# Row variance of 8192 rows: one streaming pass on VectorE, or a sum on VectorE and a square pass on ScalarE over larger DMA pieces

## The chip, the cores and the metric

The kernel runs on one core of a Trainium2 chip. The metric is the time of one execution on the device in microseconds (us). The kernel before has a median of 655.45 us over 10 runs (655.2 to 655.67). The profile quoted here is one execution, recorded by the hardware profiler.

## The reference

The input is 8192 rows of 8192 float32 values, 268.4 MB in all; the output is the (population) variance of each row, 8192 floats.

```python
def setup_inputs():
    return {"x": np.random.randn(8192, 8192).astype(np.float32)}

def reference(x):
    return np.var(x, axis=1)
```

## The kernel before

The rows are cut into 64 tiles of 128 rows, one row per partition. A tile `xt` has 128 x 8192 floats (32 KiB per partition, 4.19 MB) and lives in the pool `data` with four buffers. `issue_dma(t)` loads a tile in two halves of 128 x 4096 floats (16 KiB per partition, 2.1 MB): the first half is issued by SyncE (SP), the second by ScalarE (ACT), each from its own DMA queue (L54). A load into a buffer that was used before waits until VectorE has read the tile that lay there. The loop issues the load of tile `t` ahead of the work on tile `t - 3`.

`compute(t)` is all VectorE (DVE): 16 instructions `bn_stats` (L61), each of which reads 512 floats per partition and leaves six statistics in `st`, then one `bn_aggr` (L63), which merges the 16 groups into mean and variance `mv`. GpSimd (POOL) copies the variance into column `t` of `var_all` (L64). There is no second pass over the data.

Behind the last tile, TensorE (PE) transposes `var_all` (L74) to 64 rows of 128 values in PSUM, ScalarE copies them to SBUF (L76), and one DMA writes them out (L77). No order is written out by hand; each engine runs its instructions in the order of the program and waits on semaphores.

Of the kernel before, what the change touches and what calls it, by code (L numbers as in the profile page):

```python
# [1 line left out]

# [5 lines left out]


@with_exitstack  # L10
def kernel(
    ctx: ExitStack,
    tc: tile.TileContext,
    x: bass.AP,
    out: bass.AP,
):
    nc = tc.nc
    P = 128
    n, m = x.shape

    FMAX = nc.vector.BN_STATS_FMAX
    assert m % FMAX == 0
    nsub = m // FMAX

    assert n % P == 0
    ntiles = n // P

    x_t = x.rearrange("(t p) (s f) -> t p s f", p=P, f=FMAX)
    out_t = out.rearrange("(t p) -> t p", p=P)

    data = ctx.enter_context(tc.tile_pool(name="data", bufs=4))
    stats = ctx.enter_context(tc.tile_pool(name="stats", bufs=8))
    singles = ctx.enter_context(tc.tile_pool(name="singles", bufs=1))
    psum = ctx.enter_context(tc.tile_pool(name="psum", bufs=1, space=bass.MemoryType.PSUM))
    outp = ctx.enter_context(tc.tile_pool(name="outp", bufs=1))

    var_all = singles.tile([P, ntiles], mybir.dt.float32)
    ident = singles.tile([P, P], mybir.dt.float32)
    make_identity(nc, ident)

    dma_eng = [nc.sync, nc.scalar]

    CH = 2
    spc = nsub // CH

    xts = [None] * ntiles
    LOOK = 3

    def issue_dma(t):
        xt = data.tile([P, nsub, FMAX], mybir.dt.float32)  # L50
        for c in range(CH):
            lo = c * spc
            hi = lo + spc
            dma_eng[c % 2].dma_start(out=xt[:, lo:hi, :], in_=x_t[t, :, lo:hi, :])  # L54
        xts[t] = xt

    def compute(t):
        xt = xts[t]
        st = stats.tile([P, nsub, nc.vector.BN_STATS_DIM], mybir.dt.float32)
        for j in range(nsub):  # L60
            nc.vector.bn_stats(out=st[:, j, :], in_=xt[:, j, :])  # L61
        mv = stats.tile([P, nc.vector.BN_AGGR_DIM], mybir.dt.float32)
        nc.vector.bn_aggr(out=mv, in_=st)  # L63
        nc.gpsimd.tensor_copy(out=var_all[:, t : t + 1], in_=mv[:, 1:2])  # L64

    for t in range(ntiles):
        issue_dma(t)
        if t >= LOOK:
            compute(t - LOOK)
    for t in range(ntiles - LOOK, ntiles):  # L70
        compute(t)

    vp = psum.tile([ntiles, P], mybir.dt.float32)
    nc.tensor.transpose(vp, var_all, ident)  # L74
    vs = outp.tile([ntiles, P], mybir.dt.float32)
    nc.scalar.copy(vs, vp)  # L76
    nc.sync.dma_start(out=out_t, in_=vs)  # L77


# [1 line left out]
_INS = ['x']  # L81
_OUTS = [((8192,), 'float32')]


# [23 lines left out]
```

## Time and profile before

| what | value |
|---|---|
| median of 10 runs | 655.45 us (655.2 to 655.67) |
| time of the profiled execution | 655.2 us |
| its span, first to last instruction | 653.4 us |
| DVE busy | 636.2 us (97%) |
| ACT, POOL, PE busy | 1.5, 12.4, 0.4 us |
| moved by the DMA engines | 268.57 MB, mean 411 GB/s over the span |
| DMA queues | two, 48.5% and 48.2% of the 16 engines' span |

The span is 1.8 us shorter than the time of the same execution; that rest lies outside the instructions. A row of the list of instruction groups names the line, the engine, the operation, output and inputs with their shapes, and then the busy time in total and the mean time of one. Instructions in a row can overlap slightly, so that the distance between starts is shorter than the mean time of one.

### The profile page before, as it was taken

To read this page: it belongs to the slowest core of one execution; us is meant where nothing else is said; L and a number is where in the kernel's file an instruction comes from. 1 tells how busy PE (TensorE), PEld (TensorE's weight loads), DVE (VectorE), ACT (ScalarE), POOL (GpSimd) and SP (SyncE) were. 2 spreads that over 40 slices of the span, in tenths; PEclk is the share of its full clock that TensorE was granted. 3 is DMA by queue.
4 is the path that set the end of the run, shared out by engine and by line. 5 is a ranking of instruction groups with operands and counts; after the bars stand their busy time and mean duration, and the time that the engine had idled before them with its cause. 6 is when DMAs were issued, how large, how long until landed. Compare 5 with 4: busy or idle time off the path is not lost.

```text
span 653.4 us, 1512 instructions
## 1 busy us (share of the span) xinstructions
PE 0.4 (0%) x1; PEld 0.1 (0%) x1; DVE 636.2 (97%) x1088; ACT 1.5 (0%) x2; POOL 12.4 (2%) x70
## 2 busy tenths in 40 slices
PE   0000000000000000000000000000000000000000
PEld 0000000000000000000000000000000000000000
DVE  2999999999999999999999999999999999999997
ACT  0000000000000000000000000000000000000000
POOL 0000000000000000000000000000000000000000
DMA  9999999999999999999999999999999999999950
GB/s 369 431 429 425 430 428 428 427 430 428 425 430 429 426 428 430 427 427 429 430 425 429 429 426 426 431 428 425 430 429 426 428 429 428 426 429 429 427 227 3
DMA packets 18524, 268.57 MB, mean 411 GB/s; under 512 B 2064, under 2 KB 2128, under 8 KB 2128
## 3 DMA queue, kind: packets, MB, share of 16 engines
q1 hardware_dynamic: 9296, 134.25, 48.5%
q10 hardware_dynamic: 9216, 134.22, 48.2%
q14 instruction: 12, 0.10, 0.0%
HBM read 268.44 MB, written 0.03 MB: 411 GB/s over the span
## 4 chain that ended last, share of the span: by engine, by line
DVE 88%; DMA 6%; issue 5%; SPq 0%; PE 0%; ACT 0%; POOLq 0%; POOL 0%
DVE st L61 82%; DMA xt<-in_x_dram 6%; DVE mv L63 5%; SPq L54 0%; PE vp L74 0%; ACT vs L76 0%; POOLq L103 0%; POOL var_all L64 0%
## 5 line engine op out<-in xcount | busy, mean ns | idle before, releaser
L61 DVE BATCH_NORM_STATS2 st<-xt 128x6 f32<-128x512 f32 x1024 | 609.9, 670 | 13.4 <-DMA xt<-in_x_dram 13.4
L63 DVE BATCH_NORM_AGGREGATE mv<-st 128x2 f32<-128x96 f32 x64 | 36.4, 568 | 0.1
L64 POOL COPY var_all<-mv 128x1 f32<-128x1 f32 x64 | 11.7, 183 | 636.9 <-DVE mv L63 636.9
L76 ACT ACT_TABLE_LOAD x1 | 1.3, 1283 | 609.7 <-DMA xt<-in_x_dram 609.7
L74 PE MATMUL vp<-ident,var_all 128*64 128x128 f32 x1 | 0.4, 422 | 650.0 <-POOL var_all L64 650.0
L76 ACT COPY vs<-vp 64x128 f32<-64x128 f32 x1 | 0.3, 258 | 39.5 <-PE vp L74 39.5
masks.py:199 POOL TENSOR_SCALAR_AFFINE_SELECT ident<-ident 128x128 f32<-128x128 f32 x1 | 0.3, 292 | 0.1
L74 PEld LDWEIGHTS vp<-ident,var_all 128*64 128x64 f32 x1 | 0.1, 128 | 650.0 <-POOL var_all L64 650.0
masks.py:197 POOL MEMSET ident<- 128x128 f32 x1 | 0.2, 204 | 0.3 <-POOLq L92 0.3
L92 POOL MEMSET const-float32-0.0<- 128x1 f32 x1 | 0.1, 98 | 0.2 <-issue 0.2
L92 POOL MEMSET const-bfloat16-1.0<- 128x1 bf16 x1 | 0.1, 101 | 0.0
L92 POOL MEMSET const-uint8-127<- 128x1 uint8 x1 | 0.1, 101 | 0.0
L92 POOL MEMSET const-float32-1.0<- 128x1 f32 x1 | 0.1, 98 | 0.0
## 6 DMA issues: line engine op xcount, KB each, us to landing
xt<-in_x_dram ACTq DMA_DIRECT2D x64, 2048.0 KB, 29.2
xt<-in_x_dram SPq DMA_DIRECT2D x64, 2048.0 KB, 29.0
out_dram<-vs SPq DMA_DIRECT2D x1, 32.0 KB, 1.9
```

The source lines that it names most:

```text
L61: nc.vector.bn_stats(out=st[:, j, :], in_=xt[:, j, :])
L63: nc.vector.bn_aggr(out=mv, in_=st)
L64: nc.gpsimd.tensor_copy(out=var_all[:, t : t + 1], in_=mv[:, 1:2])
L74: nc.tensor.transpose(vp, var_all, ident)
L76: nc.scalar.copy(vs, vp)
L92: nc = _bacc.Bacc("TRN2", target_bir_lowering=False, num_devices=1)
```

## The change

- **Tiles.** Two adjacent rows lie on one partition. A tile has 128 x 16384 floats (64 KiB per partition, 8.4 MB, one contiguous piece of the input), there are 32 of them, and `data` has three buffers. Each of the tiles 0 to 29 is one DMA on SyncE's queue; ScalarE issues none. Tile 30 comes in three DMAs (row 0; the halves of row 1), tile 31 in 13 pieces: six of 2048 floats per partition, two of 1024, three of 512, two of 256.
- **Tiles 0 to 30, two passes.** VectorE forms a row's sum with one `scalar_tensor_tensor` (`row_sum`), which adds the row's two halves element by element (4096 pairs; the pairs themselves go to the PSUM tile `pair` and aren't used) and accumulates the total in `s`. ScalarE makes the mean with a small ACTIVATE, and then one Square ACTIVATE over the 8192 floats (`row_sq`) with the mean as bias, written in place over the row, which accumulates the squared deviations in `ssq`. Row 1 of tile 30 is summed by halves.
- **Their output.** PE transposes `ssq` for each of the two rows, ScalarE scales by 1/8192 into `vs`, one DMA writes 31 x 256 values.
- **Tile 31.** As before with `bn_stats` and `bn_aggr` on VectorE, except for 2048 floats of row 1: of these ScalarE forms a shifted sum and a shifted sum of squares (Identity and Square, with the mean of the first `bn_stats` group as shift), and four small GpSimd instructions turn them into one more group for `bn_aggr`. The two variances per partition, `var_last`, leave in one last DMA.

The diff, cut to its core (the removed lines are those of the functions above):

```diff
-    data = ctx.enter_context(tc.tile_pool(name="data", bufs=4))
+    x_t = x.rearrange("(t p j) f -> t p (j f)", p=P, j=J)      # J = 2, H = m // 2
+    data = ctx.enter_context(tc.tile_pool(name="data", bufs=3))
+    small = ctx.enter_context(tc.tile_pool(name="small", bufs=4))
...
+    def row_sum(s, i, src, w):
+        nc.vector.scalar_tensor_tensor(
+            out=pair[:, 0 : w // 2], in0=src[:, 0 : w // 2], scalar=1.0, in1=src[:, w // 2 : w],
+            op0=ALU.mult, op1=ALU.add, accum_out=s[:, i : i + 1])
...
+        if k == 1:
+            nc.scalar.activation(out=mean, in_=s[:, 0:1], func=ACTF.Identity, scale=1.0 / m)
...
+        nc.scalar.activation(out=src, in_=src, func=ACTF.Square, bias=mean, scale=-1.0,
+                             accum_out=ssq[:, j, t : t + 1])
...
+    for t in range(NT - 1):
...
+        if last:
+            for lo, hi in ((0, m), (m, m + H), (m + H, 2 * m)):
+                nc.sync.dma_start(out=xt[:, lo:hi], in_=x_t[t, :, lo:hi])
+        else:
+            nc.sync.dma_start(out=xt, in_=x_t[t])
+        for j in range(J):
...
+                row_sum(s, 0, rows[j], m)
+                row_sq(s, 1, rows[j], t, j)
...
+    for w in [2048] * 6 + [1024, 1024, 512, 512, 512, 256, 256]:
+        nc.sync.dma_start(out=xt[:, lo : lo + w], in_=x_t[t, :, lo : lo + w])
+        lo += w
...
+        nc.tensor.transpose(vp, ssq[:, j, 0 : NT - 1], ident)
+        nc.scalar.mul(vs[:, :, j], vp, 1.0 / m)
+    nc.sync.dma_start(out=out_tj[0 : NT - 1], in_=vs)
...
+    nc.scalar.activation(out=junk, in_=src, func=ACTF.Identity, bias=k, scale=-1.0, accum_out=s12[:, 0:1])
+    nc.scalar.activation(out=junk, in_=src, func=ACTF.Square, bias=k, scale=-1.0, accum_out=s12[:, 1:2])
...
+    for i, w in enumerate([512] * 7 + [256, 256]):
+        bn(st1, 4 + i, lo, w)
+        lo += w
+    mv1 = small.tile([P, 2], FP32, name="mv1")
+    nc.vector.bn_aggr(out=mv1, in_=st1)
+    nc.vector.tensor_copy(out=var_last[:, 1:2], in_=mv1[:, 1:2])
+        nc.sync.dma_start(out=out_last[t], in_=var_last)
```

How the instructions stand now on two engines. On VectorE, the kernel before begins with the first tile like this (`st` and `mv` are the statistics, DMAHW the semaphores of the loads), and goes on so to its end:

```order
L61 BN_STATS st<-xt 128x6 [waits DMAHW1_49]
L61 BN_STATS st<-xt 128x6 x7
L61 BN_STATS st<-xt 128x6 [waits DMAHW0_49]
L61 BN_STATS st<-xt 128x6 x7
L61 BN_STATS st<-xt 128x6 [waits DMAHW3_49]
L63 BN_AGGR mv<-st 128x2 [waits DVE_49]
```

The scheduler puts a tile's `bn_aggr` behind the first `bn_stats` of the next. The whole VectorE program of the changed kernel, from tile 0 to the end, with the statistics of tile 31's two rows as `st_474` and `st_492`:

```order
L49 SCALAR_TENSOR_TENSOR pair,s<-xt 128x4096 x61
L49 SCALAR_TENSOR_TENSOR pair,s<-xt 128x2048 x2
L101 BN_STATS st_474<-xt 128x6 x16
L128 BN_AGGR mv_491<-st_474 128x2
L101 BN_STATS st_492<-xt 128x6 x13
L135 BN_AGGR mv_517<-st_492 128x2
L136 COPY var_last<-mv_517 128x1
```

Of 1024 `bn_stats`, 29 are left, and 63 pair sums stand ahead of them. On SyncE's queue the 64 half-row loads (ScalarE's queue had 64 more) become whole tiles, and both output DMAs stand behind the last piece:

```order
-L54 DMA xt<-in_x_dram 128x4096 x64
-L77 DMA out_dram<-vs 64x128
-L103 UNCONDITIONAL_BRANCH
+L164 UNCONDITIONAL_BRANCH
+L73 DMA xt<-in_x_dram 128x16384 x30
+L71 DMA xt<-in_x_dram 128x8192
+L71 DMA xt<-in_x_dram 128x4096 x2
+L89 DMA xt<-in_x_dram 128x2048 x6
+L89 DMA xt<-in_x_dram 128x1024 x2
+L89 DMA xt<-in_x_dram 128x512 x3
+L89 DMA xt<-in_x_dram 128x256 x2
+L98 DMA out_dram<-vs 31x256
```

The row of the last output, `out_dram<-var_last 128x2`, follows these. Eight semaphores serve all loads in turn, so that a DMA also waits until the one eight places ahead of it has landed. ScalarE, which issued 64 loads and copied once, now runs 62 pairs of a mean and a Square over 8192 floats, then the two scalings into `vs`, then the two passes over 2048 floats.

More of the change, by code (lines that the diff above doesn't have):

```diff
@@ L7 @@
 from concourse._compat import with_exitstack
+FP32 = mybir.dt.float32
+ACTF = mybir.ActivationFunctionType
+ALU = mybir.AluOpType
 @with_exitstack
@@ L19 @@
     n, m = x.shape
[L21 to L29, printed above, removed]
-    data = ctx.enter_context(tc.tile_pool(name="data", bufs=4))
-    stats = ctx.enter_context(tc.tile_pool(name="stats", bufs=8))
+    F = nc.vector.BN_STATS_FMAX
+    J = 2
+    NT = n // (P * J)
+    H = m // 2
+    x_t = x.rearrange("(t p j) f -> t p (j f)", p=P, j=J)
@@ L33 @@
+    out_tj = out.rearrange("(t q) -> t q", q=P * J)
+    out_last = out.rearrange("(t p j) -> t p j", p=P, j=J)
+    data = ctx.enter_context(tc.tile_pool(name="data", bufs=3))
+    stats = ctx.enter_context(tc.tile_pool(name="stats", bufs=1))
+    small = ctx.enter_context(tc.tile_pool(name="small", bufs=4))
     singles = ctx.enter_context(tc.tile_pool(name="singles", bufs=1))
     psum = ctx.enter_context(tc.tile_pool(name="psum", bufs=1, space=bass.MemoryType.PSUM))
-    outp = ctx.enter_context(tc.tile_pool(name="outp", bufs=1))
@@ L37 @@
-    var_all = singles.tile([P, ntiles], mybir.dt.float32)
-    ident = singles.tile([P, P], mybir.dt.float32)
+    ssq = singles.tile([P, J, NT], FP32)
+    var_last = singles.tile([P, J], FP32)
+    pair = psum.tile([P, H], FP32)
+    ident = singles.tile([P, P], FP32)
     make_identity(nc, ident)
[L41 to L77, printed above, removed]
+    def row_sum(s, i, src, w):
+        nc.vector.scalar_tensor_tensor(
+            out=pair[:, 0 : w // 2], in0=src[:, 0 : w // 2], scalar=1.0, in1=src[:, w // 2 : w],
+            op0=ALU.mult, op1=ALU.add, accum_out=s[:, i : i + 1])
@@ new lines, in row_sq @@
+    def row_sq(s, k, src, t, j):
+        mean = small.tile([P, 1], FP32, name="mean")
+        if k == 1:
+            nc.scalar.activation(out=mean, in_=s[:, 0:1], func=ACTF.Identity, scale=1.0 / m)
+        else:
+            parts = small.tile([P, 4], FP32, name="parts")
+            nc.scalar.activation(out=parts[:, 0:k], in_=s[:, 0:k], func=ACTF.Identity, scale=1.0 / m,
+                                 accum_out=mean)
+        nc.scalar.activation(out=src, in_=src, func=ACTF.Square, bias=mean, scale=-1.0,
+                             accum_out=ssq[:, j, t : t + 1])
@@ new lines @@
+    for t in range(NT - 1):
+        xt = data.tile([P, J * m], FP32, name="xt")
+        rows = [xt[:, j * m : (j + 1) * m] for j in range(J)]
+        last = t == NT - 2
+        if last:
+            for lo, hi in ((0, m), (m, m + H), (m + H, 2 * m)):
+                nc.sync.dma_start(out=xt[:, lo:hi], in_=x_t[t, :, lo:hi])
+        else:
+            nc.sync.dma_start(out=xt, in_=x_t[t])
+        for j in range(J):
+            s = small.tile([P, 2], FP32, name="s")
+            if last and j == J - 1:
+                row_sum(s, 0, rows[j][:, 0:H], H)
+                row_sum(s, 1, rows[j][:, H:m], H)
+                row_sq(s, 2, rows[j], t, j)
+            else:
+                row_sum(s, 0, rows[j], m)
+                row_sq(s, 1, rows[j], t, j)
@@ new lines @@
+    t = NT - 1
+    xt = data.tile([P, J * m], FP32, name="xt")
+    lo = 0
+    for w in [2048] * 6 + [1024, 1024, 512, 512, 512, 256, 256]:
+        nc.sync.dma_start(out=xt[:, lo : lo + w], in_=x_t[t, :, lo : lo + w])
+        lo += w
+    vs = singles.tile([NT - 1, P, J], FP32)
+    for j in range(J):
+        vp = pair[0 : NT - 1, j * F : j * F + P]
+        nc.tensor.transpose(vp, ssq[:, j, 0 : NT - 1], ident)
+        nc.scalar.mul(vs[:, :, j], vp, 1.0 / m)
+    nc.sync.dma_start(out=out_tj[0 : NT - 1], in_=vs)
@@ new lines, in bn @@
+    def bn(st, i, lo, w):
+        nc.vector.bn_stats(out=st[:, i * 6 : i * 6 + 6], in_=xt[:, lo : lo + w])
+    st0 = stats.tile([P, m // F * 6], FP32, name="st0")
+    for c in range(m // F):
+        bn(st0, c, c * F, F)
+    mv0 = small.tile([P, 2], FP32, name="mv0")
+    NA = 2048
+    st1 = stats.tile([P, 13 * 6 + 3], FP32, name="st1")
+    b = 13 * 6
+    s12 = small.tile([P, 2], FP32, name="s12")
+    tmp = small.tile([P, 2], FP32, name="tmp")
+    nc.gpsimd.memset(st1[:, b : b + 1], float(NA))
@@ new lines @@
+    bn(st1, 0, m, F)
+    k = st1[:, 1:2]
+    src = xt[:, m + NA : m + 2 * NA]
+    junk = pair[:, NA : 2 * NA]
+    nc.scalar.activation(out=junk, in_=src, func=ACTF.Identity, bias=k, scale=-1.0, accum_out=s12[:, 0:1])
+    nc.scalar.activation(out=junk, in_=src, func=ACTF.Square, bias=k, scale=-1.0, accum_out=s12[:, 1:2])
+    nc.gpsimd.tensor_scalar(out=tmp[:, 0:1], in0=s12[:, 0:1], scalar1=1.0 / NA, scalar2=0.0,
+                            op0=ALU.mult, op1=ALU.add)
+    nc.gpsimd.tensor_tensor(out=st1[:, b + 1 : b + 2], in0=k, in1=tmp[:, 0:1], op=ALU.subtract)
@@ new lines @@
+    nc.gpsimd.tensor_tensor(out=tmp[:, 1:2], in0=s12[:, 0:1], in1=tmp[:, 0:1], op=ALU.mult)
+    nc.gpsimd.tensor_tensor(out=st1[:, b + 2 : b + 3], in0=s12[:, 1:2], in1=tmp[:, 1:2], op=ALU.subtract)
+    for i in range(1, 4):
+        bn(st1, i, m + i * F, F)
+    nc.vector.bn_aggr(out=mv0, in_=st0)
+    nc.gpsimd.tensor_copy(out=var_last[:, 0:1], in_=mv0[:, 1:2])
+    lo = m + 2 * NA
+    for i, w in enumerate([512] * 7 + [256, 256]):
+        bn(st1, 4 + i, lo, w)
+        lo += w
+    mv1 = small.tile([P, 2], FP32, name="mv1")
@@ L81 @@
+    nc.vector.bn_aggr(out=mv1, in_=st1)
+    nc.vector.tensor_copy(out=var_last[:, 1:2], in_=mv1[:, 1:2])
+    with nc.allow_non_contiguous_dma(reason="two values per partition"):
+        nc.sync.dma_start(out=out_last[t], in_=var_last)
 _INS = ['x']
```

## The prediction

> **What bounds the kernel now.** I read the page first, then the waits, then the timeline at both ends, then the DMA rate by stretches. The page:
>
> ```profile
> span 653.4 us, 1512 instructions
> PE 0.4 (0%) x1; PEld 0.1 (0%) x1; DVE 636.2 (97%) x1088; ACT 1.5 (0%) x2; POOL 12.4 (2%) x70
> DMA  9999999999999999999999999999999999999950
> DMA packets 18524, 268.57 MB, mean 411 GB/s; under 512 B 2064, under 2 KB 2128, under 8 KB 2128
> q14 instruction: 12, 0.10, 0.0%
> L61 DVE BATCH_NORM_STATS2 st<-xt 128x6 f32<-128x512 f32 x1024 | 609.9, 670 | 13.4 <-DMA xt<-in_x_dram 13.4
> L63 DVE BATCH_NORM_AGGREGATE mv<-st 128x2 f32<-128x96 f32 x64 | 36.4, 568 | 0.1
> L64 POOL COPY var_all<-mv 128x1 f32<-128x1 f32 x64 | 11.7, 183 | 636.9 <-DVE mv L63 636.9
> L76 ACT COPY vs<-vp 64x128 f32<-64x128 f32 x1 | 0.3, 258 | 39.5 <-PE vp L74 39.5
> masks.py:197 POOL MEMSET ident<- 128x128 f32 x1 | 0.2, 204 | 0.3 <-POOLq L92 0.3
> L92 POOL MEMSET const-float32-0.0<- 128x1 f32 x1 | 0.1, 98 | 0.2 <-issue 0.2
> out_dram<-vs SPq DMA_DIRECT2D x1, 32.0 KB, 1.9
> ```
>
> Two things look full: VectorE (97%) and the DMA engines (9 in every slice until the last two). The waits tell which one leads. VectorE waited for data only 13.4 us, three times, 13.0 of it before the first tile:
>
> ```profile
> DVE st L61 <- DMA xt<-in_x_dram: 13.4, 3, 13.0
> SPq L54 <- DVE st L61: 571.4, 60, 9.8
> ```
>
> SyncE's queue waits for VectorE to free a buffer before 60 of its loads. So VectorE sets the end. Its beginning, one tile's turn, and its end:
>
> ```profile
> 12.98 9.59 DVE L61 BATCH_NORM_STATS2 st<-xt 128x6 f32<-128x512 f32 x16 [12.98 <-DMA xt<-in_x_dram]
> ...
> 629.67 0.57 DVE L63 BATCH_NORM_AGGREGATE mv<-st 128x2 f32<-128x96 f32 x1
> ...
> 639.61 0.57 DVE L63 BATCH_NORM_AGGREGATE mv<-st 128x2 f32<-128x96 f32 x1
> 640.09 8.93 DVE L61 BATCH_NORM_STATS2 st<-xt 128x6 f32<-128x512 f32 x15
> 649.13 0.59 DVE L63 BATCH_NORM_AGGREGATE mv<-st 128x2 f32<-128x96 f32 x1
> 650.76 0.56 SPq L77 DMA_DIRECT2D out_dram<-vs  x1
> ```
>
> From one `bn_aggr` to the next is 9.94 us: a tile costs VectorE 9.94 us, 64 tiles 636 us. The DMA side by stretches (the last two columns are the busy share of the DMA engines and GB/s):
>
> ```profile
> 0.00:5.00 5.00, 0.00 (x0) 0.00 (x0) 0.00 (x0) 0.00 (x0) 0.70 (x6) 1.00 0.67 226
> 5.00:15.00 10.00, 0.00 (x0) 0.00 (x0) 2.02 (x4) 0.00 (x0) 0.00 (x0) 1.00 1.02 436
> 7.00:17.00 10.00, 0.00 (x0) 0.00 (x0) 4.02 (x7) 0.00 (x0) 0.00 (x0) 1.00 0.99 424
> 15.00:605.00 590.00, 0.00 (x0) 0.00 (x0) 589.54 (x1009) 0.00 (x0) 10.82 (x59) 1.00 1.01 428
> 628.00:629.00 1.00, 0.00 (x0) 0.00 (x0) 1.00 (x2) 0.00 (x0) 0.00 (x0) 1.00 0.86 361
> 629.00:630.00 1.00, 0.00 (x0) 0.00 (x0) 1.00 (x3) 0.00 (x0) 0.00 (x0) 1.00 0.20 82
> ```
>
> The DMA engines run at 428 GB/s from start to end with a share of 1.01, although the buffers are freed at VectorE's pace (4.194 MB in 9.94 us would be 422 GB/s). They are full in their own right and merely a little faster: 4.194 MB at 428 GB/s is 9.80 us a tile. The first stretch dates the start of the stream: 226 GB/s times 5 us is 1.13 MB, 2.64 us at 428, so it began at 2.36 us. 268.44 MB at 428 GB/s are 627.2 us, which ends at 629.6, as the last two rows show. So the gap between the bounds is small: a kernel bound by this stream saves about the 20 us between 629.6 and VectorE's last instruction, less its own tail.
>
> **The change part by part.** My sum is: start of the stream, stream, tail; it holds if the engines are covered.
>
> *VectorE, tiles 0 to 30.* 992 `bn_stats` and 62 `bn_aggr` go; 62 row sums come. No row shows a pair sum. The nearest is `bn_stats`: 15 in 8.93 us are 595 ns for 512 floats, 1.16 ns per element. A row sum of 4096 pairs at one pair per such step is 4.8 us; at two reads per pair in turn, 9.5 us. I take 4.8, and keep 9.5 as a rival. A tile of two rows then asks 9.5 us of VectorE in the 19.4 us that its data stream.
>
> *ScalarE.* Per row a mean (one small instruction: the copy of 128 elements, 258 ns) and a Square over 8192. The only ScalarE row, 258 ns for 128, would give 2.02 ns per element if it had no fixed part, 16.5 us per row. GpSimd's two fills, 204 ns for 128 and 98 ns for 1, give 0.835 ns per element, 6.8 us. GpSimd's copy of one single element takes 183 ns, so most of the 258 is fixed, and I take 6.8 + 0.26 = 7.1 us; with the mean 7.4, 14.7 us a tile of 19.4. The upper end is a rival.
>
> *Buffers.* Three instead of four, but of double size. Landing and start (0.8 us, below), first sum 4.8, mean and Square 7.4, again 7.4 (the second sum lies beneath the first Square): a buffer is free 20.4 us after its tile has streamed. By then one tile is just streaming and the load for the freed buffer is needed at 38.7 us, so 18 us are left. Costs nothing; it would cost if ScalarE needed more than 9.7 us per row.
>
> *Queue.* All loads move from two queues to SyncE's. ScalarE loses its 64 issues, SyncE has 46 for 64. Each waits for a buffer, and the two or three loads ahead of it cover that. In tile 31 a piece waits for the landing of the one eight places ahead; when piece 9 may go, pieces 2 to 8 (14.6 us of data) still stand in the queue. Nothing.
>
> *The stream.* This is the term that decides. The trace has payload packets of 16 KiB only: 18524 less the 2128 small ones and the 12 of queue 14 (instructions), 16384, or 1024 per DMA engine. At the bulk rate the stream is 627.2 us; at the best stretch's 436 it is 615.7. If the 11.5 us between are lost between packets, each costs 11.2 ns. The changed kernel, with one packet per partition and piece, has 30 x 8 + 3 x 8 + 13 x 8 = 368 packets per engine, 4.1 us: 619.8 us. The ends are 615.7 and 627.2. The bulk row is the longest, but it stands for the old packets; I take 619.8. It assumes the 436 isn't merely what a 10 us window counts at its edges; the 424 two microseconds later warns of that.
>
> The Trainium skill, page DMA: Bandwidth & Descriptors, sections Bandwidth, Measured and Where 436 GB/s comes from, puts the ceiling at 435.2 GB/s and a packet at about 10.5 ns. By it the stream would be 616.8 + 368 x 10.5 ns = 620.7 us, and the total 0.9 us above mine. The trace agrees as far as it goes: a 16 KiB packet takes 612.5 ns at 428 GB/s and 602.4 at that ceiling, 10.1 ns apart.
>
> *End of the stream.* 2.36 + 619.8 = 622.2. The rows from 628 to 630 (0.86, then 0.20) show that the engines don't end together; I add 0.5: 622.7.
>
> *Tail.* The first tile's data were through at 2.36 + 9.80 = 12.16 and VectorE began at 12.98: 0.82 us. The last `bn_stats` of 256 is 0.30, and VectorE at 1.16 ns per float against 1.19 of the stream may be one such behind, 0.30. `bn_aggr` 0.59; the copy to `var_last` as GpSimd's, 0.18; two handovers, 0.1; the output DMA from its issue to the end as before, 653.4 - 650.76 = 2.64. Together 4.9. Hidden: the output of the first 31 tiles (issued behind the last piece; 0 to 1.9 us if the last output stood behind it) and ScalarE's 2048 floats: piece 6 lands 15.4 us after tile 30's stream, two passes 3.9, four GpSimd steps 0.8, 20.1 against 21.9 for VectorE's last `bn_stats`.
>
> Sum: 622.7 + 4.9 = 627.6 us span. Outside the span 1.8 us (655.2 - 653.4): 629.4. The median of the runs is 0.25 above the profiled execution: **629.7 us**.
>
> **The rivals.**
>
> *Same rate.* The 428 is the chip's rate for any packet length here, and 436 an edge effect. For it: it holds over 590 us; 424 stands beside 436. Against: the share of 1.01 with the same packets in the best stretch. The stream stays 627.2: 7.4 more, 637.1 us.
>
> *Two reads in turn.* A pair sum takes 9.5 us. VectorE then needs 19.0 of 19.4 us a tile, still covered, but at the end it is late: tile 30's last half is summed 10.1 us after its stream, row 0 of tile 31 done at 20.1, the rest (11 `bn_stats` of 512, two of 256) at 27.3 instead of 21.9. 5.4 more: 635.1 us. Nothing in the trace of before speaks to it, since no instruction there has two inputs. The Trainium skill, page Vector Engine (DVE) Microarchitecture Reference, section Points that are easy to get wrong, says that this instruction shape with two float32 SBUF sources halves its throughput; no run so far shows it.
>
> *ScalarE becomes the bound.* With x for mean and Square of a row, the end is first landing 22.6 + first sum 4.8 + 62 x + about 9.4 (scaling, two passes, GpSimd, `bn_aggr`, output). It binds from 9.7, and the kernel is slower than before from (653.4 - 36.8) / 62 = 9.94 us. At 16.5 + 0.26 it would be 1076 us of span, about 1078. For it only the row of 258 ns taken without a fixed part; against it the 0.835 ns slope.
>
> **How the numbers follow.** The forecast has 0.66, the same rate 0.17, two reads 0.10, ScalarE 0.03, the rest (two of them together, a rate below 428) 0.04. The forecast's own range is 627.5 to 632 (stream 617.7 to 621; tail up to 1.5 longer). The range of 8 in 10 must reach the same rate and two reads: 628 to 637.6. All but ScalarE and part of the rest are faster than 654.1, by more than the 0.2% that can be told from no change: faster 0.94, within 0.2% 0.02, slower 0.04.
>
> **What would show it.** About 6,800 packets instead of 18,524; a bulk rate near 432 GB/s (428 means same rate; 18,524 packets would mean that the pieces are cut again); VectorE about half busy and waiting for DMA, its pair sums 4.8 us (9.5: two reads); ScalarE's Square near 7.1 us, the engine some 73% busy; loads issued one tile ahead of need; the last `bn_stats` 1.4 us behind the stream. The prediction falls if the DMA share drops below 9 in mid-run, which would mean a late buffer, or if the gap between the last landing and the end is far from 4.9 us.

## The result, and the profile after

The changed kernel takes 632.94 us (median of 8 runs, 632.71 to 633.38) against 655.36 us of the kernel before (29 runs). The ratio is 0.966 (95% interval 0.9651 to 0.9668): faster by 3.4%, as forecast; the time lies inside the range and 3.2 us above the 629.7 that was named. The profiled execution has a span of 631.2 us. Its page, the lines that answer to those of before:

```profile
span 631.2 us, 589 instructions
PE 0.8 (0%) x2; PEld 0.3 (0%) x2; DVE 297.2 (47%) x158; ACT 462.3 (73%) x194; POOL 1.6 (0%) x12
DMA  9999999999999999999999999999999999999995
DMA packets 6805, 268.51 MB, mean 425 GB/s; under 512 B 881, under 2 KB 1168, under 8 KB 1808
L62 ACT ACTIVATE xt<-xt,mean 128x8192 f32<-128x8192 f32 x62 | 441.5, 7121 | 2.0
L49 DVE SCALAR_TENSOR_TENSOR pair<-xt 128x4096 f32<-128x4096 f32 (+1 forms) x63 | 275.0, 4365 | 327.9 <-ACT xt L62 277.3
L57 ACT ACTIVATE mean<-s 128x1 f32<-128x1 f32 x61 | 11.9, 195 | 158.4 <-DVE pair L49 158.4
L101 DVE BATCH_NORM_STATS2 st<-xt 128x6 f32<-128x512 f32 (+1 forms) x29 | 17.3, 660 | 1.9 <-DMA xt<-in_x_dram 1.8
```

VectorE went from 97% to 47%, ScalarE from nothing to 73%, and the DMA engines are full until the last slice. No engine is near its limit any more: the stream of the input is what is left. The 277 us that VectorE waits for ScalarE (L49, last column) cost nothing by themselves: it waits for work that isn't needed earlier. In time, the bulk and the end of the stream (busy share of the DMA engines and GB/s at the right):

```profile
15.00:600.00 585.00, 0.00 (x0) 0.00 (x0) 274.65 (x123) 437.66 (x179) 0.00 (x0) 1.00 1.00 432
...
622.00:623.00 1.00, 0.00 (x0) 0.00 (x0) 1.00 (x3) 0.97 (x3) 0.52 (x3) 1.00 0.98 334
623.00:624.00 1.00, 0.00 (x0) 0.00 (x0) 1.00 (x3) 1.00 (x1) 0.00 (x0) 1.00 0.21 76
624.00:625.00 1.00, 0.00 (x0) 0.00 (x0) 1.00 (x2) 0.33 (x2) 0.19 (x1) 1.00 0.06 19
625.00:626.00 1.00, 0.00 (x0) 0.00 (x0) 1.00 (x4) 0.00 (x0) 0.00 (x0) 1.00 0.00 0
```

432 GB/s instead of 428, held over 585 us. Most DMA engines are through by 623.5 us; a share of 0.06 is one of the 16, and the last packet ends at 624.8. What comes behind the stream, in order of time:

```profile
621.34 5.01 DVE L101 BATCH_NORM_STATS2 st<-xt 128x6 f32<-128x512 f32 x9 [0.83 <-DMA xt<-in_x_dram]
626.45 0.52 DVE L135 BATCH_NORM_AGGREGATE mv<-st 128x2 f32<-128x81 f32 x1
627.00 0.15 DVE L136 COPY var_last<-mv 128x1 f32<-128x1 f32 x1
627.25 0.36 SPq L138 DMA_DIRECT2D out_dram<-var_last  x1
```

VectorE works without a gap from 621.34 to 626.35, so it ends 1.6 us behind the last packet; the output DMA then takes 631.2 - 627.25 = 3.95 us to the end. Before the change it took 2.64.

### The profile page after: what moved, and what is told of

The parts are those of the page before. It is cut to its first block, busy times and chain, and to the rows that moved or that the text cites. A ratio compares the mean times of both kernels' runs of the same rounds, so it can differ in the third digit from the quotient of the medians.

```text
span 631.2 us, 589 instructions
## 1 busy us (share of the span) xinstructions
PE 0.8 (0%) x2; PEld 0.3 (0%) x2; DVE 297.2 (47%) x158; ACT 462.3 (73%) x194; POOL 1.6 (0%) x12
## 4 chain that ended last, share of the span: by engine, by line
ACT 58%; DMA 22%; DVE 19%; issue 0%; SPq 0%; DVEq 0%
ACT xt L62 57%; DMA xt<-in_x_dram 22%; DVE pair L49 18%; ACT mean L57 1%; DVE st L101 1%; DVE mv L135 0%; SPq L73 0%; SPq L71 0%; DVE var_last L136 0%; DVEq L49 0%; DVEq L135 0%
## 5 line engine op out<-in xcount | busy, mean ns | idle before, releaser
L62 ACT ACTIVATE xt<-xt,mean 128x8192 f32<-128x8192 f32 x62 | 441.5, 7121 | 2.0
L49 DVE SCALAR_TENSOR_TENSOR pair<-xt 128x4096 f32<-128x4096 f32 (+1 forms) x63 | 275.0, 4365 | 327.9 <-ACT xt L62 277.3
L57 ACT ACTIVATE mean<-s 128x1 f32<-128x1 f32 x61 | 11.9, 195 | 158.4 <-DVE pair L49 158.4
L101 DVE BATCH_NORM_STATS2 st<-xt 128x6 f32<-128x512 f32 (+1 forms) x29 | 17.3, 660 | 1.9 <-DMA xt<-in_x_dram 1.8
L62 ACT ACTIVATION_READ_ACCUMULATOR xt<-xt,mean 128x1 f32 x62 | 11.6, 187 | 0.0
L49 DVE DVE_READ_ACCUMULATOR pair<-xt 128x1 f32 x63 | 8.9, 142 | 0.0
L119 ACT ACTIVATE pair<-xt,st 128x2048 f32<-128x2048 f32 x1 | 2.0, 1971 | 0.5 <-DMA xt<-in_x_dram 0.5
L120 ACT ACTIVATE pair<-xt,st 128x2048 f32<-128x2048 f32 x1 | 2.0, 1971 | 0.0
L128 DVE BATCH_NORM_AGGREGATE mv<-st 128x2 f32<-128x96 f32 x1 | 0.6, 589 | 0.0
```

Source lines behind the costliest of these rows:

```text
L49: nc.vector.scalar_tensor_tensor(out=pair[:, 0 : w // 2], in0=src[:, 0 : w // 2], scalar=1.0, in1=src[:, w // 2 : w], op0=ALU.mult, op1=AL ...
L57: nc.scalar.activation(out=mean, in_=s[:, 0:1], func=ACTF.Identity, scale=1.0 / m)
L62: nc.scalar.activation(out=src, in_=src, func=ACTF.Square, bias=mean, scale=-1.0, accum_out=ssq[:, j, t : t + 1])
L101: nc.vector.bn_stats(out=st[:, i * 6 : i * 6 + 6], in_=xt[:, lo : lo + w])
L119: nc.scalar.activation(out=junk, in_=src, func=ACTF.Identity, bias=k, scale=-1.0, accum_out=s12[:, 0:1])
L120: nc.scalar.activation(out=junk, in_=src, func=ACTF.Square, bias=k, scale=-1.0, accum_out=s12[:, 1:2])
```

## Experiments

All times are medians; the kernel before was run beside each group and stayed at 655.33 to 655.36 us, so the groups can be compared. Each expectation was written before its run.

**Rows apart: half the packet length, the same number of DMAs.**

```diff
+    x_a = x.rearrange("(t j p) f -> t p j f", p=P, j=J)
...
-            nc.sync.dma_start(out=xt, in_=x_t[t])
+            nc.sync.dma_start(out=xt.rearrange("p (j f) -> p j f", j=J), in_=x_a[t])
...
```

> The changed kernel, but the two rows of a partition are 128 rows apart in the input (tiles 0 to 30), so that each tile is still one DMA, of two 32 KiB packets per partition instead of one of 64. Theory A (each packet costs the DMA engines about 10 ns, whatever its length): 240 packets more per engine, +2.4 us, 635.3 us against 632.9. Theory B (the rate of 432 GB/s comes from one queue or from whole-tile DMAs, packet length does not matter): 632.9.

Measured: 635.35 us (635.04 to 635.53), +2.4. Theory A, to the tenth. Its bulk rate is 431 GB/s with 10645 packets.

**Quarters: the old packet length on the one queue.**

```diff
-            nc.sync.dma_start(out=xt, in_=x_t[t])
+            for lo in range(0, J * m, 4096):
+                nc.sync.dma_start(out=xt[:, lo : lo + 4096], in_=x_t[t, :, lo : lo + 4096])
```

> The changed kernel, but tiles 0 to 29 come in four DMAs of 16 KiB per partition each, the packet length of the kernel before, all from SyncE's queue. Theory A (10 ns per packet): 720 data packets and 90 completions more per engine, +7.3 to +8.2 us, 640 to 641 us, bulk rate 428 GB/s as before the change. Theory B (one queue instead of two gave the rate): 632.9 us and 432 GB/s.

Measured: 639.41 us (639.27 to 639.52), +6.5, below the 7.3 to 8.2 of theory A, far from B. The bulk rate is back at that of before:

```profile
5.00:100.00 95.00, 0.00 (x0) 0.00 (x0) 40.43 (x18) 63.47 (x26) 0.00 (x0) 1.00 1.00 428
100.00:600.00 500.00, 0.00 (x0) 0.00 (x0) 229.11 (x102) 377.28 (x154) 0.00 (x0) 1.00 1.01 428
```

The landing itself can be read from SyncE's issues in tile 31: the issue of piece 8 waits for tile 30's last piece. These three rows are of the changed kernel, of rows apart, and of quarters:

```profile
604.15 0.33 SPq L89 DMA_DIRECT2D xt<-in_x_dram  x1
```
```profile
606.57 0.33 SPq L90 DMA_DIRECT2D xt<-in_x_dram  x1
```
```profile
611.71 0.33 SPq L90 DMA_DIRECT2D xt<-in_x_dram  x1
```

+2.42 us for 240 packets more per engine is 10.1 ns each; +7.56 us for 720 is 10.5 (90 completions included in the time, not in the count). The 10.5 is too high: before this landing all five instruction packets of quarters have crossed a DMA engine, but only three of the changed kernel's five, and each holds an engine up (see the late second piece below). Over the whole time, with five in both, quarters is 6.47 us slower, 9.0 ns a packet. In rows apart three stand ahead of the landing, as in the changed kernel. So packet length makes the rate, at 9 to 10 ns a packet. The 1.1 us that quarters gives back behind this point comes up below.

**An eighth of the work.**

```diff
...
-                row_sum(s, 0, rows[j], m)
-                row_sq(s, 1, rows[j], t, j)
+                row_sum(s, 0, rows[j][:, 0:1024], 1024)
+                row_sq(s, 1, rows[j][:, 0:1024], t, j)
```

> The changed kernel with one eighth of the work on tiles 0 to 30: sums and squares run over 1024 floats of each row only (the rest of the row is left out of the result). Theory (the stream alone sets the time, the engines are covered): 632.9 us within 0.4. Rival (ScalarE's late release of buffers, or VectorE's late start on tile 31, still costs something): 1 to 3 us faster.

Measured: 632.83 us (632.50 to 632.94), the same. ScalarE at 15% and VectorE at 10% buy nothing: in the changed kernel both lie wholly under the stream, and their traffic doesn't slow it.

**The new loads alone, with the old work on VectorE.**

```diff
...
+        nc.sync.dma_start(out=xt, in_=x_t[t])
+        for j in range(J):
...
+                nc.vector.bn_stats(out=st[:, c * 6 : c * 6 + 6], in_=xt[:, lo : lo + F])
...
+            nc.vector.bn_aggr(out=mv, in_=st)
...
```

> The new loads alone: 32 tiles of two rows per partition, one DMA of 64 KiB per partition each on SyncE's queue, three buffers, but bn_stats and bn_aggr on VectorE for every row as before the change. Theory (VectorE at 9.94 us per row was the bound, and a tile of double size starts it 10 us later): 22.7 + 636.2 + about 4.6 of tail = 663.5 us span, 665 us, slower than before. Rival (the larger pieces are the gain): below 640 us.

Measured: 670.09 us (669.99 to 670.13), 2.25% slower than before (ratio 1.0225, 1.0211 to 1.0238). The direction and its cause are as expected, the size was 5 us short:

```profile
L73 DVE BATCH_NORM_STATS2 st<-xt 128x6 f32<-128x512 f32 x1024 | 609.8, 674 | 22.6 <-DMA xt<-in_x_dram 22.6
L75 DVE BATCH_NORM_AGGREGATE mv<-st 128x2 f32<-128x96 f32 x64 | 37.1, 580 | 3.2
```

VectorE waits 22.6 us for the first tile of double size instead of 13.0, and never again. The rest is that a row cost it 10.03 us (from 22.57 to its last `bn_aggr` at 664.09 plus 0.6, over 64) and not 9.94. Of these 5.8 us, 3.2 are idle time ahead of `bn_aggr` (0.1 before); here half of them stand directly behind their own `bn_stats`. The other 2.6 are open. The larger pieces alone are a loss; they pay only once VectorE is off the bound.

**Tail: finer last pieces.**

```diff
-    for w in [2048] * 6 + [1024, 1024, 512, 512, 512, 256, 256]:
+    for w in [2048] * 6 + [512] * 7 + [256] * 2:
```

> The changed kernel, with the last 4096 floats of tile 31 in seven pieces of 512 and two of 256 instead of two of 1024, three of 512, two of 256 (VectorE's groups are the same). Theory (the last bn_stats ended 1 us later than the landing because VectorE got 1024 floats at once and then had 5.0 us of work without a gap): the first 512 land 0.6 us earlier, 0.16 us is paid for 16 more packets, 632.4 us. Rival (the last landing alone sets the end): 632.9 to 633.1.

Measured: 632.51 us (632.11 to 632.85), -0.43, as the theory had it, though the two kernels' runs overlap slightly. The row that carries it: VectorE starts the last 4096 floats 0.9 us earlier and ends 0.6 us earlier (20.47 + 5.32 against 21.34 + 5.01, with 600 us left out), although tile 30 landed at the same time (604.19 against 604.15). The profiled execution is the fastest of its five, and 0.3 us of its lead lies behind the issue of the output.

```profile
620.47 5.32 DVE L101 BATCH_NORM_STATS2 st<-xt 128x6 f32<-128x512 f32 x9 [0.25 <-DMA xt<-in_x_dram]
```

**Tail: the last output as two rows of 512 bytes.**

```diff
+    x_l = x.rearrange("(t j p) f -> t j p f", p=P, j=J)
...
-    nc.vector.tensor_copy(out=var_last[:, 1:2], in_=mv1[:, 1:2])
...
-        nc.sync.dma_start(out=out_last[t], in_=var_last)
+    nc.tensor.transpose(lp, var_last.rearrange("p j s -> p (j s)"), ident)
+    nc.scalar.copy(ls, lp)
+    nc.sync.dma_start(out=out_last[t], in_=ls[1 : 2 * J : 2, :])
```

> The changed kernel, with tile 31's two rows per partition 128 rows apart in the input, so that its variances can leave as two rows of 512 bytes: a transpose on PE and a copy on ScalarE (0.42 and 0.26 us, about 0.85 with handovers, less 0.25 for VectorE's copy that goes) stand ahead of the output DMA. Theory (128 writes of 8 bytes took the output DMA 1.3 us longer than the 512-byte rows before the change): from issue to the end 2.6 us instead of 3.95, 632.2 us in all. Rival (the output DMA is late for another reason): 3.95 stays, 633.5 us.

Measured: 632.11 us (631.82 to 632.18), -0.83, against 632.2 expected. The span is 630.4, so the DMA takes 2.54 us from its issue to the end:

```profile
627.17 0.37 PE L135 MATMUL pair<-ident,var_last 128*4 128x128 f32 x1 [7.69 <-DVE var_last L133]
627.58 0.25 ACT L137 COPY ls<-pair 4x128 f32<-4x128 f32 x1 [3.10 <-PE pair L135]
627.86 0.71 SPq L138 DMA_DIRECT2D out_dram<-ls  x1
```

**Tail: without the first output DMA.**

```diff
-    nc.sync.dma_start(out=out_tj[0 : NT - 1], in_=vs)
```

> The changed kernel without the output DMA of tiles 0 to 30 (their variances are left out of the result). Theory of small writes: the last output DMA still takes 3.95 us from issue to the end, 632.9 us. Rival (the last output waits behind the first one's 31 rows of 1 KB): 2.6 us, 631.6 us.

Measured: 632.94 us (632.43 to 633.24), and 631.4 - 627.49 = 3.91 us from issue to end. The last output isn't held up by the first; its 128 writes of 8 bytes are what takes longer than rows of 512 bytes. Over all traces it is 3.6 to 4.3 us from issue to the end for the 128 writes (eight kernels) and 2.54 to 2.58 for the two rows of 512 bytes (three kernels); the 64 rows of 512 bytes before the change took 2.64. Whether 128 writes are slow by their size alone or by their number too wasn't separated.

**The late second piece.** SyncE's issues in the changed kernel also give the landings of the first pieces of tile 31 (each issue waits for the piece eight ahead):

```profile
604.15 0.33 SPq L89 DMA_DIRECT2D xt<-in_x_dram  x1
606.63 0.33 SPq L89 DMA_DIRECT2D xt<-in_x_dram  x1
610.10 0.33 SPq L89 DMA_DIRECT2D xt<-in_x_dram  x1
612.58 0.33 SPq L89 DMA_DIRECT2D xt<-in_x_dram  x1
615.07 0.33 SPq L89 DMA_DIRECT2D xt<-in_x_dram  x1
```

Pieces come every 2.48 us, but the second took 3.47, and all later ones keep that 1.0 us. A piece has landed when all 16 DMA engines have reported their part, and the trace has each report: fifteen of them come about 2.5 us behind those of the first piece, and only one comes 3.5 behind. An instruction packet of 8 KB crosses one DMA engine at 608 us; these are the rows of the DMA queues from 608 to 609 us, and from 622 to 623:

```profile
q14 instruction: 1, 0.01, 2.1%
```
```profile
q14 instruction: 1, 0.01, 2.3%
```

First try, more instructions in SyncE's program:

```diff
-            nc.sync.dma_start(out=xt, in_=x_t[t])
+            for lo, hi in ((0, m), (m, 2 * m)) if 1 <= t <= 8 else ((0, 2 * m),):
+                nc.sync.dma_start(out=xt[:, lo:hi], in_=x_t[t, :, lo:hi])
```

> The changed kernel, with tiles 1 to 8 in two DMAs each, which puts eight instructions more into SyncE's program ahead of the end, and 64 packets more per engine on the stream. Theory A (the 1.0 us that the second piece of tile 31 landed late is an instruction fetch of SyncE over a DMA engine): the second piece lands 2.5 us behind the first instead of 3.5, and the fetch is seen earlier; +0.65 us for the packets, less up to 1.0: 632.6 to 633.6 us. Theory B (the delay belongs to that piece): 3.5 us stay, 633.6 us.

Measured: 633.25 us (632.72 to 633.86), and 3.46 us between the landings. By itself that speaks for theory B. But the trace shows that the test missed: a packet moved from 622 to 590 us, which is probably SyncE's, and the packet of 608 stayed (609), so that one seems to belong to another engine. The next run therefore shifted VectorE's and ScalarE's programs:

```diff
...
+    for _ in range(40):
+        nc.vector.memset(scr, 1.0)
+    for _ in range(40):
+        nc.scalar.copy(scr2, scr)
     for t in range(NT - 1):
```

> The changed kernel, with 40 tiny instructions each on VectorE and ScalarE ahead of the first tile, where both engines wait for data anyway; they shift the place at which these engines' programs fetch their next instructions (an 8 KB packet on one DMA engine at 608 us, while the second piece of tile 31 is under way). Theory A (that fetch is the 1.0 us by which the second piece lands late): the piece lands 2.5 us behind the first instead of 3.5 and the end comes up to 1.0 us earlier, 631.9 to 632.5 us. Rival (a fetch costs the same wherever it falls): the interval is 2.5 but every landing before it is later, 632.9 us. Theory B (the delay isn't the fetch): 3.5 and 632.9 us.

Measured: 632.59 us (632.24 to 632.63), -0.35. The packet left 608 us (the nearest are one between 510 and 520 and one at 622), and the gap is gone:

```profile
604.99 0.33 SPq L95 DMA_DIRECT2D xt<-in_x_dram  x1
607.48 0.33 SPq L95 DMA_DIRECT2D xt<-in_x_dram  x1
609.95 0.33 SPq L95 DMA_DIRECT2D xt<-in_x_dram  x1
```

The second piece lands 2.47 us behind the first: the fetch was the delay. But tile 30 landed at 604.99 instead of 604.15, so most of it only moved ahead of that point, and the last piece of all landed at 625.07 instead of 625.22: the rival, not theory A. The 0.35 us is at the edge of what these runs tell; of the 0.4 us between the two traces most lies behind the issue of the output (3.7 us to the end instead of 3.95), where the fetch has no part. Quarters, whose trace has no instruction packet behind 490 us, has regular pieces too, which is where it gave back about 1 us.

**The changes of the tail together, and with the shift.**

> The two changes of the tail together: 512-float pieces at the end, and the last output as two 512-byte rows. If they add up (-0.43 and -0.83 us measured alone), 631.7 us; if the second hides the first, 632.1.

Measured: 632.08 us (631.92 to 632.28): no better than the 512-byte output alone, as the second of the two expectations has it, but not for its reason. In this program tile 30 landed 0.6 us later than in that one (604.89 against 604.31), and why is open. Counted from that landing, VectorE ended 0.5 us sooner than in that one, so the finer pieces did their part and the late stream took it back.

> The two changes of the tail and the 40 tiny instructions on each of VectorE and ScalarE at the start: 631.7 us if the place of the fetch does not matter, down to 630.7 if it does.

Measured: 631.59 us (631.50 to 631.70), ratio 0.9638 (0.9624 to 0.9651). It is the best version that ran, 1.35 us under the changed kernel. Behind its stream nothing large is left: a span of 629.9 us with the last DMA issued at 627.35.

## Why the prediction was right, point by point

- **The bound.** VectorE before, the stream after: shown from both sides. The new loads without the new work are slower than before (670.1), and the new work at an eighth of its size is no faster (632.8). Quarters divides the gain: with the old packet length the new work brings 15.9 of the 22.4 us (655.33 to 639.41), longer packets the other 6.5.
- **VectorE's sum.** 4.8 us were taken from `bn_stats`, 4.43 measured for 4096 pairs (4433 ns in the list by shape). The rival of two reads in turn is out: 1.08 ns per pair. The rule of the Trainium skill (Vector Engine (DVE) Microarchitecture Reference, Points that are easy to get wrong), by which this shape halves its throughput, doesn't show in this trace.
- **ScalarE.** 7.1 us per Square were taken, 7.12 measured; 73% busy, as worked out. The slope of GpSimd's fills was the right row, the copy of 258 ns without a fixed part the wrong one: the Square over 8192 (7121 ns) and the pass over 2048 (1971) give 0.838 ns per float and 0.25 us fixed. That another engine's slope would fit so closely was in part luck, since no row before tied the two together.
- **Buffers and queue.** Never late: the DMA share holds at 9 in every slice until the last.
- **The stream, the deciding term.** The mechanism was right: a cost per packet, 9 to 10 ns by the two experiments, 11.2 taken. The rival of the same rate is out. The size was off by the other factor: the 436 GB/s of a 10 us stretch was taken as the rate without any packets' cost. At the measured 432 GB/s the stream is 621.4 us, not 619.8: 1.6 us. The prediction had named that weakness and gone on. How far so short a stretch can be off is seen in the changed kernel, whose rate over 585 us is 432 and which shows 446 from 5 to 15 us:

```profile
5.00:15.00 10.00, 0.00 (x0) 0.00 (x0) 0.00 (x0) 0.00 (x0) 0.00 (x0) 1.00 1.03 446
```

  The figures of the Trainium skill (DMA: Bandwidth & Descriptors, Bandwidth), which gave 620.7 us, were nearer. The 10.5 ns of the Trainium skill lies a little above the 9 to 10 of the runs.
- **The end of the stream and the tail, the other mis-sized terms.** The last packet ends at 624.8 instead of 622.7: 1.6 us is the rate, the other 0.5 the slowest DMA engine, which ends 1.0 us behind 2.36 + 621.4 = 623.8 where 0.5 was allowed. From there to the end of the last `bn_stats` it is 1.6 us against 1.4; VectorE was thought one `bn_stats` of 256 behind and got 1024 floats at once (finer pieces start it 0.9 us earlier), but the data reached it sooner than the 0.82 us taken. From the last `bn_stats` to the issue 0.9 us, as forecast. The output DMA took 3.95 us instead of 2.64, because the price was taken from rows of 512 bytes and these are of 8: 1.3 us. Together 1.6 + 0.5 + 0.2 + 1.3 = 3.6 us, by which the span exceeds the forecast. The sign that the prediction set for itself, 4.9 us from the data to the end, came out at 6.4.
- **A term at nothing: instruction packets.** The prediction let the old stream end at 629.6 us and counted its 12 instruction packets as nothing. One of the 16 engines went on until 638:

```profile
630.00:632.00 2.00, 0.00 (x0) 0.00 (x0) 2.00 (x5) 0.00 (x0) 0.18 (x1) 1.00 0.06 25
636.00:638.00 2.00, 0.00 (x0) 0.00 (x0) 2.00 (x5) 0.00 (x0) 0.00 (x0) 1.00 0.06 25
638.00:640.00 2.00, 0.00 (x0) 0.00 (x0) 2.00 (x4) 0.00 (x0) 0.00 (x0) 1.00 0.00 0
```

  The engines' reports show how: the slowest falls back by 0.6 to 1.0 us at nine of the 12 packets, and is 8.7 us behind the median engine in the last load. That load landed at 638.5 us, less than 1 us before VectorE came to its tile. The changed kernel has 589 instructions for 1512 and five such packets, which hit more than one engine, and its slowest engine is 1.7 us behind at the end. So the saving came out near the forecast partly by luck: with the old 8.7 us, the end would be at about 640 us (an estimate from these two traces), outside the range. No run changed the number of instruction packets alone.
- **The forecast's own range**, 627.5 to 632, missed by 0.9 us. It allowed the stream 1.2 us more and the tail 1.5 more; rate, slowest engine and tail came to 3.6. The time lies in the range of 628 to 637.6 only because that was stretched to hold two rivals, same rate and two reads, which the runs rule out.

## What to carry to other kernels

When two resources are nearly full, the trace of before already shows what the second one allows: here 428 GB/s without a dip against a reader at 422, and the distance between the two ends was most of the gain. Look for the end of the slowest DMA engine, not of the average one. Price a stream by its longest row, not its best stretch, and then correct it by the packet count; take a DMA's price from rows of its own size. A larger piece is worth nothing, or less, as long as the engine that reads it is the bound, since it also delays the first piece.

## What the runs showed of the hardware that was not expected

- An output DMA of 128 writes of 8 bytes ended 3.6 to 4.3 us behind its issue, one of two rows of 512 bytes 2.54 to 2.58 us, with the same bytes in all.
- An instruction fetch, one packet of 8 KB on one of the 16 DMA engines, made a 1 MB piece land 1.0 us late, and the pieces behind it too. Forty tiny instructions on each of two engines in idle time moved it elsewhere. In the kernel before, such packets left one DMA engine 8.7 us behind the others at the end.
- One queue serves the DMA engines as well as two: with packets of 16 KiB both give 428 GB/s. With 64 KiB it is 432.
